# An encoder layer whose inputs are handed over turned: x, mem and Wq transposed on the host, parameters packed, the residual loaded into its accumulator

## The chip, the cores and the metric

The kernel runs on one core of a Trainium2 chip. The metric is the device time of one execution in microseconds (us). A profile of one execution tells when each engine worked: TensorE (PE; its weight loads are PEld), VectorE (DVE), ScalarE (ACT), GpSimd (POOL), and the DMA queues, of which that of SyncE (SP) issues nearly all transfers.

## The reference

One layer of a bidirectional encoder on 2048 tokens of 1024 numbers, all in float32:

```
u = rmsnorm(x) * g_mix;  P = u @ W_in                        # 1024 -> 3600 columns
hyena group: 3-tap conv of P; two long convolutions by FFT with filters made by a small sine network
mLSTM group: 3-tap conv, SiLU; chunkwise scan in both directions; sigmoid output gate
h = x + concat(groupnorm(hyena), groupnorm(mlstm)) @ w_out
h = h + softmax((rmsnorm(h) Wq)(rmsnorm(mem) Wk)^T / 16) (rmsnorm(mem) Wv) Wo     # 4 heads, 256 rows of mem
h = h + relu(rmsnorm(h) @ W1)^2 @ W2
out = rmsnorm(h)
```

x and mem come with one token per row, the weights with one input channel per row.

## The kernel before

**Products.** A product of two float32 matrices is done as three faster products of their parts (`mm3`, L293): each operand is split into a high part (a copy on ScalarE that rounds, L300) and a low part (a subtraction on VectorE, L301). A "bank" is one accumulator of 128 by 512 in TensorE's output memory; a bank of the projection takes 8 times 3 matmuls. Plain float32 matmuls, slower, are used for the FFT stages and the filters.

**Channels on partitions.** For a product TensorE wants the channels along the partitions. x and mem are stored with tokens along them, so they are turned. `prep` (L425) goes over row tiles of 128 tokens: `prep_load` (L395) loads one, `prep_norm` (L404) squares it on ScalarE with a running sum, makes 1/rms in a chain of small VectorE operations (`rsqrt`, L144) and multiplies by it and by the gain, `prep_turn` (L416) turns it in eight transposes on TensorE (L420) and splits the result into xh and xl. Half of x (1024 tokens) fits at a time, so it is prepared three times: first half, second half, first half again. `turned` (L331) does the same for Wq, four transposes (L341) for each of 16 pieces.

**Stages.** `program` (L1638) sets the order. `sweep` (L512) projects the hyena and q, k columns with the weights as they come from `stream` (L347), which loads and splits one weight pair ahead; each bank is copied, convolved on ScalarE and VectorE, turned back (L576) and stored. Between its banks the sweep pops the generator of the next preparation (L546, L550). `filters` (L158) is woven between the sweep's steps and opens a pool of its own; `hyena` (L638), `natural` (L605), `mlstm` (L771) and `memproj` (L458: products of mem with Wk and Wv, and of these with Wq and Wo) follow in the same way. `attention` (L1061) goes over four chunks of 512 tokens: w_out product, residual, norm, scores, softmax, second product. At the beginning of a chunk `residual` (L1131) loads x by rows, turns it on TensorE (`turn`, L1103, and L1106) and copies it into `acc`; `finish` (L1141) adds each bank to it, and L1243 stores it for the later stages. The feed-forward part comes last.

**Order.** The instructions are put in order by a scheduler of the framework that simulates the engines; `keep_in_program_order` exempts single instructions. Each engine and each DMA queue works strictly in its order, so a wait holds what stands behind it.

Of the kernel before, what the change touches and what calls it, by code (L numbers as in the profile page):

```python
# [9 lines left out]
F32 = mybir.dt.float32  # L10
# [86 lines left out]

class Prog:
    def __init__(self, ctx, tc, a):
# [17 lines left out]
        self.prepq = None  # L117
        self.rbp = cp.tile([128, 16], F32, name="rbp")
        self.ps = ctx.enter_context(tc.tile_pool(name="ps", bufs=1, space=PSUM))
# [38 lines left out]
    def filters(self):  # L158
# [3 lines left out]
        with tc.tile_pool(name="f_sb", bufs=1, side="right") as sb:  # L162
            def ta(bufs=7):
                return sb.tile([128, 2, CH], F32, tag="a", name="a", bufs=bufs)

            def tb(bufs=8):
                return sb.tile([128, CH], F32, tag="b", name="b", bufs=bufs)

            w1 = sb.tile([66, 128], F32, name="w1")
            w2 = sb.tile([128, 128], F32, name="w2")  # L170
            w3 = sb.tile([128, 2, CH], F32, name="w3")
            f1 = sb.tile([128, 2, 128], F32, name="f1")
            nc.vector.memset(w1, 0.0)
            nc.vector.memset(w2, 0.0)
            nc.gpsimd.dma_start(out=w1[0:33, 0:64], in_=a["hy_filt_w1"][0])
            nc.gpsimd.dma_start(out=w1[33:66, 64:128], in_=a["hy_filt_w1"][0])
            nc.gpsimd.dma_start(out=w2[0:64, 0:64], in_=a["hy_filt_w2"][0])
            nc.gpsimd.dma_start(out=w2[64:128, 64:128], in_=a["hy_filt_w2"][0])
            par = sb.tile([128, 4], F32, name="par")
            for i, n in enumerate(("b1", "freq1", "b2", "freq2")):  # L180
                src = a["hy_filt_" + n].rearrange("o c -> c o")
                for h in range(2):
                    nc.gpsimd.dma_start(out=par[64 * h:64 * h + 64, i:i + 1], in_=src)
            w3v = a["hy_filt_w3"][0].rearrange("k (o r c) -> r k o c", o=2, r=2)
            for h in range(2):
                nc.gpsimd.dma_start(out=w3[64 * h:64 * h + 64], in_=w3v[h])
            nc.gpsimd.dma_start(out=f1, in_=a["c_f1"])

            def sine(dst, src, b, fr):
                u, k = tb(), tb()  # L190
                nc.vector.tensor_scalar(u, src, par[:, b:b + 1], par[:, fr:fr + 1], ALU.add, ALU.mult)
# [6 lines left out]
                nc.vector.tensor_scalar(u, u, -PI_F, PI_F, ALU.max, ALU.min)  # L198
                nc.scalar.activation(dst, u if len(dst.shape) == 2 else u.rearrange("p (q j) -> p q j", j=16), AF.Sin)

            hid = sb.tile([128, 16, 128], F32, name="hid")
            for c in range(4):
# [7 lines left out]
                sine(hid1, p1, 0, 1)  # L210
# [8 lines left out]
            def windows(j2):  # L219
# [3 lines left out]
                for r in range(2):  # L223
                    nc.sync.dma_start(out=w[r], in_=wv[r, :, 2 * j2:2 * j2 + 2])
# [40 lines left out]
            def blocks(o, i):  # L265
                p, k = divmod(2 * i, 16)
                dm = sb.tile([128, 2, 128], F32, tag="dm", name="dm", bufs=3)
                nc.sync.dma_start(out=dm, in_=a["c_dm"][:, 2 * i:2 * i + 2])
# [6 lines left out]
            for n, (o, i) in enumerate(order):  # L275
                if True:
# [9 lines left out]
                    nc.sync.dma_start(out=hd[o, 2 * i:2 * i + 2].rearrange("k l c -> l k c"), in_=hs)  # L286

    def column(self, ap, n, name):
        t = self.cp.tile([128, n], F32, name=name, tag=name)
        self.nc.gpsimd.dma_start(out=t, in_=ap.rearrange("o (k p) -> p (o k)", p=128))  # L290
        return t
# [7 lines left out]
    def split(self, hi, lo, src):  # L299
        self.nc.scalar.copy(hi, src)  # L300
        self.nc.vector.tensor_tensor(lo, src, hi.bitcast(F32), ALU.subtract)  # L301
# [10 lines left out]
    def weights(self, pool, w, n, kc=4, bufs=2, nbufs=2):  # L312
# [12 lines left out]
        for k0 in range(0, kt, kc):  # L325
            nat = pool.tile([128, kc, n], F32, tag="wn", name="wn", bufs=nbufs)
            nc.sync.dma_start(out=nat, in_=w[128 * k0:128 * (k0 + kc), :].rearrange("(k p) c -> p k c", p=128))
            self.split(hi[:, k0:k0 + kc], lo[:, k0:k0 + kc], nat)
        return hi, lo

    def turned(self, pool, w):  # L331
        nc = self.nc
        hi = pool.tile([128, 2, 1024], F32R, tag="wh", name="wh", bufs=2)
        lo = pool.tile([128, 2, 1024], F32R, tag="wl", name="wl", bufs=2)
        for i in range(4):
            nat = pool.tile([128, 2, 256], F32, tag="wn", name="wn", bufs=3)
            nc.sync.dma_start(out=nat, in_=w[256 * i:256 * i + 256, :].rearrange("(k p) c -> p k c", p=128))
            pt = self.mm()
            for m in range(2):
                for k in range(2):  # L340
                    nc.tensor.transpose(pt[:, 256 * m + 128 * k:256 * m + 128 * k + 128],  # L341
                                        nat[:, k, 128 * m:128 * m + 128], self.ident)
            ds = slice(256 * i, 256 * i + 256)
            self.split(hi[:, :, ds], lo[:, :, ds], pt.rearrange("p (m c) -> p m c", m=2))
        return hi, lo

    def stream(self, pool, items, **kw):  # L347
        nxt = None
        for i in range(len(items) + 1):
            cur = nxt  # L350
            if i < len(items):
                w, n = items[i]
                nxt = self.turned(pool, w) if n is None else self.weights(pool, w, n, **kw)
            if cur is not None:
                yield cur
# [3 lines left out]
    def inproj_open(self, es):  # L359
# [9 lines left out]
        self.g_mix = self.bcast(sb, a["norm_mix_g"], D, "g_mix")  # L369
        self.turned_to = lambda h: (self.xh[:, 4 * h:4 * h + 4], self.xl[:, 4 * h:4 * h + 4])  # L370
        self.xh = sb.tile([128, 8, 1024], F32R, name="xh")
        self.xl = sb.tile([128, 8, 1024], F32R, name="xl")
        self.cw = sb.tile([128, 3, 20], F32, name="cw")
        self.cb = sb.tile([128, 20], F32, name="cb")
        for i in range(3):
            nc.gpsimd.dma_start(out=self.cw[:, i, 0:12], in_=a["hy_conv_w"][:, i].rearrange("o (k p) -> p (o k)", p=128))
            nc.gpsimd.dma_start(out=self.cw[:, i, 12:20], in_=a["ml_conv_w"][:, i].rearrange("o (k p) -> p (o k)", p=128))
        nc.gpsimd.dma_start(out=self.cb[:, 0:12], in_=a["hy_conv_b"].rearrange("o (k p) -> p (o k)", p=128))
        nc.gpsimd.dma_start(out=self.cb[:, 12:20], in_=a["ml_conv_b"].rearrange("o (k p) -> p (o k)", p=128))
        self.gb = sb.tile([128, 16], F32, name="gb")  # L380
        nc.gpsimd.dma_start(out=self.gb, in_=a["ml_gate_b"].broadcast_to([128, 16]))
        self.carry = sb.tile([128, 20, 17], F32, name="carry")
# [5 lines left out]
        second = [(a["xa_wq"][0][:, h], None) for h in hs] + [(a["xa_wo"][0][h, :], 1024) for h in hs]  # L388
# [4 lines left out]
        self.wst = self.stream(sb, items, kc=2, nbufs=3)  # L393

    def prep_load(self, src, first, i):  # L395
        sb = self.isb
        if first and i % 3:
            xn = sb.tile([128, 1042], F32, tag=("P", "cv")[i % 3 - 1], name="xn", bufs=2)[:, 0:D]
        else:
            xn = sb.tile([128, D], F32, tag="xn", name="xn", bufs=2)  # L400
        self.nc.sync.dma_start(out=xn, in_=src)
        return xn

    def prep_norm(self, xn, gain):  # L404
        nc, sb = self.nc, self.isb
        ss = sb.tile([128, 2], F32, tag="ss", name="ss", bufs=2)
        for h in range(2):
            junk = sb.tile([128, 512], F32, tag="st", name="junk", bufs=3)
            nc.scalar.activation(junk, xn[:, 512 * h:512 * h + 512], AF.Square, accum_out=ss[:, h:h + 1])
        ms = sb.tile([128, 1], F32, tag="ms", name="ms", bufs=2)  # L410
        nc.vector.tensor_tensor(ms, ss[:, 0:1], ss[:, 1:2], ALU.add)
        nc.vector.tensor_scalar(ms, ms, 1.0 / D, EPS, ALU.mult, ALU.add)
        rv = self.rsqrt(sb, ms, "xr")
        nc.vector.scalar_tensor_tensor(xn, xn, rv, gain, ALU.mult, ALU.mult)

    def prep_turn(self, xn, t):  # L416
        for h in range(2):
            p = self.mm().rearrange("p (k t) -> p k t", k=4)
            for k in range(4):
                self.nc.tensor.transpose(p[:, k], xn[:, 512 * h + 128 * k:512 * h + 128 * k + 128], self.ident)  # L420
            hi, lo = self.turned_to(h)
            ts = slice(128 * t, 128 * t + 128)
            self.split(hi[:, :, ts], lo[:, :, ts], p)

    def prep(self, src, gain, first=False):  # L425
        n = src.shape[0] // 128
        ahead = 5 if first else 1
        q = []
        for i in range(n + ahead):
            if i < n:  # L430
                xn = self.prep_load(src[128 * i:128 * i + 128, :], first, i)
                q.append(xn)
# [1269 lines left out]
```

## Time and profile before

| | |
|---|---|
| median of 3 runs | 3382.24 us (3379.86 to 3386.33) |
| the profiled execution | 3383.48 us, its span 3381.8 us |
| TensorE busy | 3194.3 us, 94% |
| VectorE, ScalarE, GpSimd busy | 60%, 44%, 38% |
| mean granted TensorE clock | 0.979 |

The span runs from the first to the last instruction. "Busy" of TensorE is modelled, since matmuls overlap. A row of a group gives line, engine, operation, output and input by the program's names, shapes, count, busy time, mean length of one in ns, and the idle time of the engine just before such instructions with what ended it. A row of the timeline gives start and length in us. A row of a wait gives the total in us, the number of times and the longest.

### The profile page before, as it was taken

What the parts mean: (1) busy time and instruction counts of PE and PEld (TensorE: products, weight loads), DVE (VectorE), ACT (ScalarE), POOL (GpSimd) and SP (SyncE); (2) the same over time, 40 slices, a digit from 0 to 9 for tenths busy, and PEclk for the clock granted to TensorE, in tenths of its full rate; (3) what the DMA queues carried; (4) which work ended last, traced back from release to release, by engine and by line L of the source; (5) the groups of instructions that cost most, each with busy time, mean ns of one, the idle gap of its engine ahead of it and who ended that gap; (6) DMA issues with size and microseconds to landing.
All of it is one profiled execution on the core that took longest, in us unless ns stands there. A gap on an engine that the chain in (4) does not pass through costs nothing.

```text
span 3381.8 us, 46860 instructions
## 1 busy us (share of the span) xinstructions
PE 3194.3 (94%) x15671; PEld 2550.0 (75%) x15671; DVE 2042.5 (60%) x3711; ACT 1492.4 (44%) x2884; POOL 1269.8 (38%) x894
## 2 busy tenths in 40 slices
PE   6999999999898888799999999999999999999997
PEld 5646666677676788688887997788788887888876
DVE  7685225524546755777766554755855576555695
ACT  4344435523454235444444444555655543333335
POOL 2131001200222314544424012876766564434482
PEclk9999999999999999999999999999999999999998
DMA  5366889996998579857657444765654475444434
GB/s 165 117 208 206 286 282 256 271 325 238 241 240 279 172 229 273 275 154 231 184 162 253 147 132 161 224 205 179 207 167 158 147 244 171 128 140 135 133 94 159
DMA packets 480749, 674.55 MB, mean 199 GB/s; under 512 B 41738, under 2 KB 256848, under 8 KB 479484
## 3 DMA queue, kind: packets, MB, share of 16 engines
q1 hardware_dynamic: 478904, 668.70, 63.4%
q0 software_dynamic: 1600, 2.86, 0.4%
q8 instruction: 124, 2.03, 0.3%
q14 instruction: 117, 0.96, 0.1%
q10 hardware_dynamic: 4, 0.00, 0.0%
HBM read 452.23 MB, written 219.18 MB: 199 GB/s over the span
## 4 chain that ended last, share of the span: by engine, by line
PE 43%; DVE 7%; DMA 5%; issue 3%; POOL 2%; ACT 1%; SPq 1%; DVEq 0%; ACTq 0%; POOLq 0%
PE mm L295 9%; PE mm L297 9%; PE mm L296 9%; PE hy L297 5%; PE hy L295 4%; PE hy L296 4%; DVE wl L301 1%; DVE bl L1292 1%; POOL acc L1500 1%; DMA rw<-rows 1%; PE hy L1106 1%; DMA wr<-xs 1%; DMA wn<-in_x_dram 1%; DMA va<-vd 1%; DVE acc L1542 0%
## 5 line engine op out<-in xcount | busy, mean ns | idle before, releaser
L301 DVE TENSOR_TENSOR wl<-wn,wh 128x512 fp32r<-128x512 f32 (+1 forms) x352 | 274.6, 813 | 144.4 <-ACT wh L300 143.8
L1292 DVE TENSOR_TENSOR bl<-wr,bh 128x512 fp32r<-128x512 f32 x213 | 234.8, 1108 | 134.6 <-ACT bh L1291 132.2
L1291 ACT CAST ah<-w 128x512 fp32r<-128x512 f32 x284 | 176.2, 622 | 298.9 <-PE hy L296 152.7
L300 ACT CAST wh<-wn 128x512 fp32r<-128x512 f32 (+1 forms) x352 | 202.1, 617 | 216.2 <-PE mm L296 80.0
L295 PE MATMUL mm<-xh,wh 128*128 128x512 f32 x640 | 276.4, 432 | 8.7 <-ACT P L542 7.5
L739 POOL TENSOR_TENSOR b<-b,a 128x512 f32<-128x512 f32 x64 | 88.8, 1387 | 502.1 <-ACT b L737 201.1
L296 PE MATMUL mm<-xl,wh 128*128 128x512 f32 x640 | 266.4, 416 | 0.1
L297 PE MATMUL mm<-xh,wl 128*128 128x512 f32 x640 | 264.3, 413 | 0.3 <-DVE wl L301 0.3
L1292 DVE TENSOR_TENSOR al<-w,ah 128x512 fp32r<-128x512 f32 x236 | 226.9, 963 | 59.9 <-ACT ah L1291 59.7
L1291 ACT CAST bh<-wr 128x512 fp32r<-128x512 f32 x232 | 143.4, 621 | 244.3 <-PE mm L297 180.1
L297 PE MATMUL mm<-bh,al 128*128 128x512 f32 x576 | 224.4, 392 | 8.3 <-DVE al L1292 5.7
L295 PE MATMUL mm<-bh,ah 128*128 128x512 f32 x576 | 226.0, 392 | 0.0
L296 PE MATMUL mm<-bl,ah 128*128 128x512 f32 x576 | 225.0, 391 | 0.0
L295 PE MATMUL mm<-act,wh 128*128 128x512 f32 x512 | 201.4, 397 | 6.0 <-ACT wh L300 6.0
L296 PE MATMUL mm<-act,wh 128*128 128x512 f32 x512 | 203.0, 397 | 0.0
L297 PE MATMUL mm<-act,wl 128*128 128x512 f32 x512 | 201.1, 396 | 0.0
L1149 POOL TENSOR_TENSOR ssum<-ssum,sq 128x512 f32<-128x512 f32 x56 | 80.7, 1440 | 269.7 <-ACT sq L1148 268.2
L295 PE MATMUL hy<-bh,ah 128*128 128x512 f32 x448 | 175.2, 391 | 0.0
L296 PE MATMUL hy<-bl,ah 128*128 128x512 f32 x448 | 174.6, 390 | 0.0
L297 PE MATMUL hy<-bh,al 128*128 128x512 f32 x448 | 174.6, 390 | 0.0
L295 PEld LDWEIGHTS mm<-xh,wh 128*128 128x128 f32 x640 | 122.4, 191 | 56.7 <-issue 18.0
L295 PE MATMUL hy<-xh,ah 128*128 128x512 f32 x384 | 152.8, 398 | 7.6 <-ACT ah L1291 6.8
(379 smaller groups left out, 9021.1 us busy)
## 6 DMA issues: line engine op xcount, KB each, us to landing
wr<-hc SPq DMA_DIRECT2D x224, 256.0 KB
w<-in_ff_w_dram SPq DMA_DIRECT2D x176, 256.0 KB
a<-hd SPq DMA_DIRECT2D x128, 256.0 KB
hc<-t SPq DMA_DIRECT2D x128, 256.0 KB
wn<-in_w_in_dram SPq DMA_DIRECT2D x104, 256.0 KB
hc<-q SPq DMA_DIRECT2D x96, 256.0 KB
fs<-a SPq DMA_DIRECT2D x32, 512.0 KB
a<-fs SPq DMA_DIRECT2D x32, 512.0 KB
```

The lines of the kernel that those rows point to most:

```text
L295: mm(ps, lh, rh, start=start, stop=False)
L296: mm(ps, lh, rl, start=False, stop=False)
L297: mm(ps, ll, rh, start=False, stop=stop)
L300: self.nc.scalar.copy(hi, src)
L301: self.nc.vector.tensor_tensor(lo, src, hi.bitcast(F32), ALU.subtract)
L739: nc.gpsimd.tensor_tensor(xt, xt, hi[:, m], ALU.mult)
L1106: nc.tensor.transpose(pt[:, 128 * k:128 * k + 128], yn[:, 128 * k:128 * k + 128], self.ident)
L1149: nc.gpsimd.tensor_tensor(ssum, ssum, sq, ALU.add)
L1291: self.nc.scalar.copy(hi, src)
L1292: eng.tensor_tensor(lo, src, hi.bitcast(F32), ALU.subtract)
L1500: nc.gpsimd.tensor_tensor(v, v, ms[2 * tp + n], ALU.mult)
```

## The change

The host hands over, beside x and mem, their transposes `x_t` and `mem_t`, and Wq only transposed; it packs all gains, convolution weights and biases into one array of 128 by 192 (`par`) and the filter network's weights into one of 128 by 1280 (`fw`).

- x is loaded with channels on partitions (`x_load`) and needs no turning. 1/rms of a token, which is now needed along the free dimension, is made into a diagonal matrix (`diagonal`) and spread over all partitions by one matmul with ones (`spread`); VectorE multiplies by gain and 1/rms (`gained`), and the pieces are split.
- The sums of squares come for the first 512 tokens from the turned tiles (squares added on VectorE, four matmuls with a column of ones). For the other tokens and mem they come from row tiles that are loaded beside (`row_stats`), once, in steps popped between the first banks; the third preparation reuses them.
- `x_first` writes the beginning out by hand, with most of the order pinned; the second 512 tokens are written in the middle of the first bank (`self.mid`).
- The pool of the filters is opened first, and its tiles hold the first weights and x.
- Wq goes through the ordinary `weights`.
- `residual` is one DMA of 128 by 2048 numbers straight into `acc`, which is one tile for all four chunks; in the first chunk it stands behind the turning of the mLSTM rows.
- Tiles of P and cv are 1088 wide in place of 1042; some loads of the filters are kept in program order.

```diff
-    def prep_turn(self, xn, t):
-        for h in range(2):
-            p = self.mm().rearrange("p (k t) -> p k t", k=4)
-            for k in range(4):
-                self.nc.tensor.transpose(p[:, k], xn[:, 512 * h + 128 * k:512 * h + 128 * k + 128], self.ident)
...
+    def spread(self, dg, pin=False):
+        n = dg.shape[1]
+        p = self.mm()
+        d = self.nc.tensor.matmul(p[:, 0:n], self.ones, dg, start=True, stop=True)
...
+        rb = self.isb.tile([128, 512], F32, tag="rb", name="rb", bufs=2)
+        self.nc.scalar.copy(rb[:, 0:n], p[:, 0:n])
+        return rb[:, 0:n]
+
+    def gained(self, x, g, rb):
+        return self.nc.vector.scalar_tensor_tensor(x, x, g, rb, ALU.mult, ALU.mult)
+
+    def scaled(self, x, k0, gain, rb, hi, lo):
+        for k in range(x.shape[1]):
+            self.gained(x[:, k], gain[:, k0 + k:k0 + k + 1], rb)
+        self.split(hi, lo, x)
...
+    def x_chunk(self, c):
+        rb = self.spread(self.diagonal(self.rx[:, 4 * c:4 * c + 4]))
+        xs = [self.x_load(c, 0)]
+        for j in range(4):
+            if j < 3:
+                xs.append(self.x_load(c, j + 1))
+            to = slice(2 * j, 2 * j + 2), slice(512 * (c % 2), 512 * (c % 2) + 512)
+            self.scaled(xs.pop(0), 2 * j, self.g_mix, rb, *(t[(slice(None),) + to] for t in (self.xh, self.xl)))
+            yield
...
+    def x_first(self):
...
+        for k in range(8):
+            sq = sb.tile([128, 512], F32, tag="st", name="sq", bufs=3) if k else ssum
+            pin(nc.scalar.activation(sq, x0[k], AF.Square))
+            if k:
+                nc.vector.tensor_tensor(ssum, ssum, sq, ALU.add)
+        p = self.mm()
+        for t in range(4):
+            nc.tensor.matmul(p[:, t:t + 1], ssum[:, 128 * t:128 * t + 128], self.ones[:, 0:1], start=True, stop=True)
+        self.inv_rms(self.rx[:, 0:4], p[:, 0:4])
+        dg = self.diagonal(self.rx[:, 0:4])
...
+        rb = self.spread(dg)
...
+        write(x0, c0, rb, between)
+
+        def rest():
+            write(x1, c1, self.spread(later[0], True))
+            w1 = self.weights(sb, *self.items[1], kc=2, nbufs=3, pin=True)
+            self.wst = self.stream(sb, self.items[2:], w1, kc=2, nbufs=3)
+        self.mid = rest
+        for _ in range(9):
+            yield
+        for c in (2, 3):
+            yield from self.row_stats(self.rx[:, 4 * c:4 * c + 4], self.a["x"][512 * c:512 * c + 512])
+        yield from self.row_stats(self.rm, self.a["mem"])
...
-        second = [(a["xa_wq"][0][:, h], None) for h in hs] + [(a["xa_wo"][0][h, :], 1024) for h in hs]
+        second = [(a["xa_wq_t"][h, :], 1024) for h in hs] + [(a["xa_wo"][0][h, :], 1024) for h in hs]
...
             def residual(h):
-                q = [rows(a["x"], 512 * c + 128 * t, h) for t in range(2)]
-                for t in range(4):
-                    xn = q.pop(0)
-                    if t < 2:
-                        q.append(rows(a["x"], 512 * c + 128 * (t + 2), h))
-                    self.copy(acc[:, 4 * h:4 * h + 4, 128 * t:128 * t + 128], turn(xn))
+                src = a["x_t"].rearrange("(k p) t -> p k t", p=128)[:, 4 * h:4 * h + 4, 512 * c:512 * c + 512]
+                nc.sync.dma_start(out=acc[:, 4 * h:4 * h + 4], in_=src)
...
                     half = [gemm(w, i, y, None, range(4)) for i in range(2)]
+                    next(mix)
                     residual(0)
                     residual(1)
-                    next(mix)
```

More of the change, by code (lines that the diff above doesn't have):

```diff
@@ L117, in __init__ @@
         self.prepq = None
+        self.mid = None
         self.rbp = cp.tile([128, 16], F32, name="rbp")
+        par = self.par = cp.tile([128, 192], F32, name="par")
+        nc.scalar.dma_start(out=par, in_=a["par"])
+        self.g_mix, self.g_mem, self.gx, self.gf = (par[:, 8 * i:8 * i + 8] for i in range(4))
+        self.cw = par[:, 32:92].rearrange("p (i c) -> p i c", i=3)
+        self.cb, self.gb = par[:, 92:112], par[:, 112:128]
         self.ps = ctx.enter_context(tc.tile_pool(name="ps", bufs=1, space=PSUM))
@@ L310, in bcast, with weights @@
         return t
-    def weights(self, pool, w, n, kc=4, bufs=2, nbufs=2):
+    def weights(self, pool, w, n, kc=4, bufs=2, nbufs=2, pin=False):
         nc = self.nc
@@ L327, in weights, with stream @@
             nc.sync.dma_start(out=nat, in_=w[128 * k0:128 * (k0 + kc), :].rearrange("(k p) c -> p k c", p=128))
-            self.split(hi[:, k0:k0 + kc], lo[:, k0:k0 + kc], nat)
+            self.split(hi[:, k0:k0 + kc], lo[:, k0:k0 + kc], nat, pin)
         return hi, lo
[L331 to L349, printed above, removed]
-            cur = nxt
[L351 to L355, printed above, removed]
+    def stream(self, pool, items, cur, **kw):
+        for w, n in items:
+            nxt = self.weights(pool, w, n, **kw)
+            yield cur
+            cur = nxt
+        yield cur
     NAT_AT = (0, 2, 4)
@@ L368, in inproj_open @@
         sb = self.isb = es.enter_context(tc.tile_pool(name="i_sb", bufs=1))
[L369 to L370 removed]
         self.xh = sb.tile([128, 8, 1024], F32R, name="xh")
         self.xl = sb.tile([128, 8, 1024], F32R, name="xl")
[L373 to L382, printed above, removed]
+        small = sb.tile([128, 448], F32, name="small")
+        self.carry = small[:, 0:340].rearrange("p (c t) -> p c t", c=20)
+        self.rx, self.rm = small[:, 340:356], small[:, 356:358]
         win = a["w_in"][0]
@@ L416, in prep_turn @@
-    def prep_turn(self, xn, t):
-        for h in range(2):
-            p = self.mm().rearrange("p (k t) -> p k t", k=4)
-            for k in range(4):
[L420 to L432, printed above, removed]
-            if i >= ahead:
-                xn = q.pop(0)
-                self.prep_norm(xn, gain)
-                self.prep_turn(xn, i - ahead)
-                yield
+        self.items = items
```

253 lines of the change are left out of this document (182 added, 71 removed).

## The prediction

> **What bounds the kernel now.** I read the page first, then the stretches around the places that the diff touches, then the waits, then the start instruction by instruction. The page:
>
> ```profile
> span 3381.8 us, 46860 instructions
> ...
> PE 3194.3 (94%) x15671; PEld 2550.0 (75%) x15671; DVE 2042.5 (60%) x3711; ACT 1492.4 (44%) x2884; POOL 1269.8 (38%) x894
> ...
> PE 43%; DVE 7%; DMA 5%; issue 3%; POOL 2%; ACT 1%; SPq 1%; DVEq 0%; ACTq 0%; POOLq 0%
> ```
>
> TensorE is the bound: 94% of the span, 187.5 us idle in all, and the largest share of the chain that ends last. An edit pays if it takes work from TensorE's stream or if it shortens a stretch in which TensorE waits. The stretches (columns: PE, PEld, DVE, ACT, POOL busy with instruction counts, granted TensorE clock, DMA share, GB/s):
>
> ```profile
> 0.00:60.00 60.00, 33.03 (x135) 24.59 (x136) 41.24 (x154) 28.33 (x62) 17.70 (x31) 0.97 0.72 203
> 150.00:300.00 150.00, 147.31 (x510) 76.75 (x509) 112.51 (x238) 64.01 (x125) 45.26 (x25) 1.00 0.53 181
> 800.00:900.00 100.00, 86.14 (x400) 60.05 (x399) 60.14 (x162) 45.06 (x97) 11.81 (x9) 0.91 0.87 260
> 1100.00:1150.00 50.00, 41.72 (x237) 32.83 (x235) 49.52 (x129) 9.03 (x22) 26.22 (x18) 0.90 0.55 189
> 1150.00:1280.00 130.00, 113.30 (x885) 109.39 (x884) 65.11 (x213) 42.01 (x82) 14.23 (x17) 0.93 0.68 207
> 1400.00:1450.00 50.00, 38.32 (x211) 32.31 (x210) 26.30 (x70) 17.15 (x45) 13.42 (x12) 0.86 0.82 253
> 1600.00:1640.00 40.00, 36.47 (x192) 30.23 (x191) 25.20 (x57) 16.46 (x42) 13.96 (x11) 0.96 0.66 211
> 1790.00:1830.00 40.00, 31.76 (x145) 25.04 (x144) 20.88 (x28) 14.92 (x26) 19.50 (x14) 0.91 0.99 329
> ```
>
> The first 60 us hold 27 us of TensorE's idle time. The stretch 150 to 300 is full of TensorE work. The other six are the places where x is prepared a second time (800), mem is prepared (1100), Wq is turned (1150) and the residual is turned (1400, 1600, 1790): in all of them TensorE has gaps and a granted clock below 1.
>
> **What goes from TensorE.** The groups (busy, mean ns of one, idle before) and the 64 turns of Wq:
>
> ```profile
> L420 PE MATMUL mm<-ident,xn 128*128 128x128 f32 x208 | 33.2, 304 | 30.6 <-DVE xr_t L153 16.5 <-DVE hr_t L154 5.8 <-DVE xr_t L154 4.7
> L1106 PE MATMUL hy<-ident,wn 128*128 128x128 f32 x256 | 39.4, 296 | 19.2 <-DMA wn<-in_x_dram 9.8 <-DMA wn<-yh 7.6 <-DMA wn<-ym 1.4
> L734 PE MATMUL hy<-a,dm 128*128 128x512 f32 x128 | 68.6, 622 | 8.7 <-DMA a<-zs 6.8 <-issue 1.9
> L341 PE MATMUL mm<-ident,wn x64: 270/273/448, 1172.3 to 1271.2; 128*128 128x128 f32 x64
> ```
>
> All 208 transposes of L420 go (3 times 64 for x, 16 for mem), all 64 of L341, and 128 of the 256 of L1106 (4 chunks, 2 halves, 4 rows, 4 each): 400. The means overlap, since transposes are pipelined; a run of twelve took 1.47 us (row at 52.46 below), 0.12 each, less the tail of the last, so I count 0.11 each in a full stream: 44 us. By busy time (33.2/208) it is 0.16 each, 64 us; that is the upper bound.
>
> What comes: seven matmuls that spread 1/rms over the partitions, six of 512 columns and one of 256, in f32. L734 is that operation: 64 matmuls (two instructions each) in 68.6 us, 1.07 each, so 7 us in all, and four tiny ones. Net 37 us off TensorE.
>
> **1. The start (edits: x handed over turned, pool of the filters opened first, packed parameters).** TensorE's stream, and when ScalarE could square the row tiles of x:
>
> ```profile
> 10.16 1.94 PE L420 MATMUL mm<-ident,xn 128*128 128x128 f32 x8 [10.16 <-DVE xr_t L153]
> ...
> 30.75 1.38 PE L295 MATMUL mm<-xh,wh 128*128 128x512 f32 x1
> ...
> 44.38 0.50 PE L295 MATMUL mm<-xh,wh 128*128 128x512 f32 x1 [2.78 <-ACT P L542]
> 44.72 0.39 PE L296 MATMUL mm<-xl,wh 128*128 128x512 f32 x1
> 44.95 0.39 PE L297 MATMUL mm<-xh,wl 128*128 128x512 f32 x1
> ...
> 52.46 1.47 PE L420 MATMUL mm<-ident,xn 128*128 128x128 f32 x12
> ...
> 74.19 1.91 PE L576 MATMUL mm<-ident,cv 128*63 128x128 f32 x16
> ```
>
> ```profile
> 4.35 0.63 ACT L409 ACTIVATE junk<-xn 128x512 f32<-128x512 f32 x1 [2.26 <-DMA xn<-in_x_dram]
> ...
> 13.96 0.63 ACT L409 ACTIVATE junk<-xn 128x512 f32<-128x512 f32 x1 [2.54 <-DMA xn<-in_x_dram]
> ```
>
> ```profile
> DMA packets 1043, 3.03 MB, mean 216 GB/s; under 512 B 312, under 2 KB 312, under 8 KB 1043
> ```
>
> At 74.19 the first four banks of the projection are done (matmuls of a bank start 0.23 apart, 24 of them are 5.6 us, four are 22.4) and the first result is turned: the mark that I compare. The new first chunk is four loads of 512 KB, as large as the four row tiles whose fourth was there at 13.96, while 3.03 MB moved in the first 14 us. The packed weights of the filters (655 KB on POOL's queue) stand where the 512 KB of the broadcast gain stood. So x is whole at about 14 us again. Then, in a chain:
>
> ```profile
> 5.72 0.16 DVE L411 TENSOR_TENSOR ms<-ss 128x1 f32<-128x1 f32 x1 [4.34 <-ACT junk L409]
> 5.92 0.15 DVE L412 TENSOR_SCALAR ms<-ms 128x1 f32<-128x1 f32 x1
> ...
> 52.66 0.81 DVE L191 TENSOR_SCALAR b<-hy,par 128x512 f32<-128x512 f32 x1 [1.84 <-PE hy L212]
> ...
> 58.36 0.43 DVE L198 TENSOR_SCALAR b<-b 128x512 f32<-128x512 f32 x1
> ```
>
> ```profile
> L301 DVE TENSOR_TENSOR wl<-wn,wh 128x512 fp32r<-128x512 f32 (+1 forms) x352 | 274.6, 813 | 144.4 <-ACT wh L300 143.8
> L301 DVE TENSOR_TENSOR xl<-mm,xh 128x512 fp32r<-128x512 f32 x48 | 31.8, 683 | 4.0 <-ACT xh L300 3.9
> L414 DVE SCALAR_TENSOR_TENSOR xn<-xn,xr_y,g_mix 128x1024 f32<-128x1024 f32 x24 | 32.2, 1343 | 0.7 <-DMA g_mix<-in_norm_mix_g_dram 0.4
> L300 ACT CAST xh<-mm 128x512 fp32r<-128x512 f32 x48 | 26.4, 589 | 14.5 <-PE mm L420 14.4
> ```
>
> Last square 0.6, last add 0.7, four column sums 0.6 (no row; an estimate from the transposes, 0.24 each at 10.16, less overlap), thirteen small VectorE operations 0.2 apart (rows at 5.72 and 5.92) 2.5, four diagonals 0.8 (an estimate, 0.2 each as for the small ones), the spread matmul 1.1 (L734) and its copy 0.6 (L300), first gain 0.7 (half of L414), first copy 0.6: 8.2, so the first real matmul stands at 22 to 23 in place of 30.75. From there VectorE sets the pace: a gain and a subtraction, two at 0.68, for each of 16 pieces, 22 us, and in between the sums of the second chunk (fourteen small ones and a diagonal, 3.5) and one set of the sine (3.5, six operations between L191's 0.81 and L198's 0.43). 22.5 + 29 = 51.5, plus the filters' f32 matmuls that also stand before 74.19 (about four, 1.07 each): 56. Gain 18, of which 7 are the 64 transposes. Bounds: VectorE at 0.81 for each piece and another sine set, 68 (gain 6); everything overlapped but the chain, 48 (gain 26). The pinned instructions only say which goes first; the pinned window loads wait behind pieces of x in the same buffers, but the filters need them late.
>
> **2. x, second half (150 to 300).** 64 transposes, 7 us, less two spreads, 2.1: 5. TensorE is busy for 98% there, so it counts in full; bounds 3 and 8 (at 0.16 each). VectorE has less: a chunk now costs it 16 pieces, 11 to 13 us, where four row tiles cost four chains of 2.5, four multiplications of 1.34 and eight subtractions of 0.68, 21 us.
>
> **3. x, first half again (800 to 900).** The same 5; above it up to 8 more of the 14 us idle there, below it nothing, as DMA is at 0.87. I take 5.
>
> **4. mem (1100 to 1150).** 16 transposes less half a spread: 1. The statistics move to the start's idle ScalarE, so the chain in front of the transposes goes; its wait was 5.8 (row L420, hr_t). I take 4 together, bounds 0 and 9.
>
> **5. Wq handed over turned (1150 to 1280).** 7 us of transposes, and the waits in front of them:
>
> ```profile
> PE mm L341 <- DMA wn<-in_xa_wq_dram: 7.8, 5, 3.2
> PE mm L341 <- DVE pad L823: 2.5, 1, 2.5
> PE mm L341 <- DVE cb L910: 1.9, 1, 1.9
> ```
>
> The DMA's wait can move to the copies of the same weights, the VectorE ones (4.4) go with the transposes: 11, bounds 3 and 19.
>
> **6. The residual by DMA.** 128 transposes, 14 us, and 32 copies on ScalarE and VectorE. The waits for in_x (9.8, row L1106) go as far as nothing follows them; 2048 KB a chunk come as before, in two loads that wait for the accumulator to be free:
>
> ```profile
> 1577.97 0.37 SPq L1243 DMA_DIRECT2D h<-acc  x1
> ...
> 1611.53 0.32 SPq L1243 DMA_DIRECT2D h<-acc  x1
> ```
>
> The second half is free after the store at 1611.53, and its load is needed five banks (28 us) later. TensorE can run four banks ahead, 22 us, before a late first half stops it, but the add that waits holds VectorE's queue, with the next weights' subtractions behind it. I take 14 plus half the waits, 5, less 3 for that: 16. Bounds 6 (a 3 us stall at each chunk) and 26.
>
> The small parameter loads that are packed, and the tiles at equal offsets, I cost at nothing: the only wait for one of them in the rows above is 0.4 on VectorE (L414, g_mix). If the packed load came late, the first gain would be late by as much; it has 20 us.
>
> In sum 18 + 5 + 5 + 4 + 11 + 16 = 59. The profiled execution took 3383.5 (its span and 1.7 around it), 1.2 above the median of the runs, by which every time below is lowered: 3383.5 - 59 - 1.2 = 3323. All low bounds, 18, give 3364; all high ones, 101, give 3281.
>
> A rule that speaks against the change: VectorE's subtraction takes 813 ns from SBUF and 683 from PSUM (rows L301), and the change makes some 104 pieces (16 for each of six and a half chunks) read twice from SBUF. The Trainium skill, page "SBUF — State Buffer", section "Who interferes with whom", says that a VectorE instruction with two SBUF inputs contends with a GpSimd one that reads SBUF, and that the later one is blocked altogether. The trace agrees in the sign. By that rule 104 times 0.13, 14 us, come back if all were on the path, and the sum is 45; by the rows VectorE is the pace only at the start, where POOL is idle, so I leave it at 59.
>
> **The rivals.**
> A, as above: 3323, own range 3305 to 3345, chance 0.60.
> B, hidden anyway: in the stretches at 800 and 1100 to 1280 other things (DMA at 0.87, 0.68) set the time, and VectorE's pace eats the start: 6 + 5 + 0 + 0 + 3 + 16 = 30, 3352, chance 0.18. For it: TensorE idles there already. Against: the waits named are those of the transposes.
> C, the clock comes back too: the six stretches with transposes lose (1 - clock) times their length: 9 + 5 + 9 + 7 + 1.6 + 3.6 = 35. Eight transposes at 10.16 took 0.24 each, twice the 0.12 at 52.46. If turning lowers the clock, 59 + 35 = 94: 3288, chance 0.12. Against: most of the loss stands beside waits that stay.
> The Trainium skill, page "TensorE: Matmul & The Clock Gate", section "Part 4: PE-mode transpose", states this rule: transposes don't count as activity for the clock gate. The rate at 52.46 speaks against it.
> D, slower: the loads into the accumulator are issued on SP's queue right behind the first store, and the second waits there for the second store, 33.6 us later; behind it stand the weights. With one pair of weights in hand (two banks, 11.2) TensorE stops for 22.4 at each of three boundaries, 67: 3390. It decides from 22 us at each (59 + 7 over 3). Chance 0.05. For it: the queue is in order. Against: the load stands behind the first bank in the program.
> E, no change, the same with stops of some 20 us: 0.05. That the transposes stay in can't be: no call of them is left.
>
> **The numbers.** Faster means below 3375.5, slower above 3389: 0.2% (6.8 us) is about what a measurement of this kernel can tell from no change. A, B and C are faster, 0.90; E 0.05; D 0.05. The range takes in A, B and most of C and leaves out D and E: 3288 to 3366.
>
> **What would show it.** TensorE's instructions fall by about 390. First projection matmul at 21 to 24, the first turned result (74.19 now) at 48 to 68. No wait in front of TensorE for x, xr or Wq chains; in the stretch of the residual, TensorE's idle time down by 5 to 10 us and the loads of x into the accumulator landing before the bank that needs them. SP's queue not held for over 10 us by those loads. I am wrong if the mark at the start moves by under 6 us, or if idle time in front of the projections of mem, Wq or the first banks of a chunk grows by what the transposes took.

## The result, and the profile after

The changed kernel takes 3352.95 us (median of 6 runs, 3346.61 to 3358.46), the kernel before beside it 3381.05 (6 runs): ratio 0.9911, 95% interval 0.9894 to 0.9928. It is faster by 28 us, about half of the 59 forecast. The profiled execution took 3358.12 us, 25.4 less than the profiled one of before. The page of the changed kernel (span, busy time by engine, the chain by engine):

```profile
span 3356.4 us, 45646 instructions
...
PE 3171.6 (94%) x15293; PEld 2518.0 (75%) x15293; DVE 2039.8 (61%) x3469; ACT 1469.7 (44%) x2811; POOL 1262.9 (38%) x868
...
PE 69%; DMA 15%; DVE 9%; issue 3%; ACT 2%; SPq 1%; POOL 1%; DVEq 0%; ACTq 0%; POOLq 0%
```

TensorE has 378 instructions less, but only 22.7 us less of busy time where 37 were counted, and it idles as long as before (184.8 against 187.5 us). The transfers' share of the chain has gone from 5% to 15%. TensorE's stream at the start of the changed kernel, and VectorE's last subtraction for x there:

```profile
24.00 0.79 PE L323 MATMUL mm<-xh,wh 128*128 128x512 f32 x1 [2.11 <-ACT xh L483]
...
28.30 0.63 PE L323 MATMUL mm<-xh,wh 128*128 128x512 f32 x1
28.73 1.90 PE L226 MATMUL hy<-b,fw 66*128 66x512 f32 x2
...
35.04 2.08 PE L230 MATMUL hy<-b,fw 128*128 128x512 f32 x2 [3.24 <-ACT b L217]
37.46 0.79 PE L323 MATMUL mm<-xh,wh 128*128 128x512 f32 x1 [0.35 <-ACT xh L483]
...
39.63 1.91 PE L440 MATMUL mm<-dg,ones 128*128 128x512 f32 x2
...
43.90 0.51 PE L325 MATMUL mm<-xh,wl 128*128 128x512 f32 x1
...
67.64 1.91 PE L706 MATMUL mm<-ident,cv 128*63 128x128 f32 x16
```

```profile
53.52 0.68 DVE L485 TENSOR_TENSOR xl<-a,xh 128x512 fp32r<-128x512 f32 x1
```

The first projection matmul has come forward from 30.75 to 24.00, and the mark (first turned result) by about as much, 6.6 us, from 74.19 to 67.64. The same stretches as in the prediction, in the changed kernel (same columns):

```profile
0.00:60.00 60.00, 35.98 (x109) 24.07 (x110) 45.44 (x104) 30.43 (x58) 1.97 (x8) 0.91 0.53 186
...
1150.00:1280.00 130.00, 121.82 (x970) 118.72 (x969) 72.35 (x220) 48.05 (x91) 18.66 (x19) 0.97 0.72 224
1400.00:1450.00 50.00, 42.19 (x210) 35.01 (x210) 37.05 (x66) 22.93 (x55) 18.83 (x15) 0.93 0.67 207
1600.00:1640.00 40.00, 39.01 (x185) 32.60 (x186) 30.00 (x55) 17.39 (x43) 17.83 (x13) 0.91 0.61 189
1790.00:1830.00 40.00, 31.44 (x156) 26.82 (x154) 30.18 (x28) 17.23 (x30) 26.73 (x19) 0.91 0.76 239
```

Where the time came from is seen best by asking when the same piece of work starts in both traces. Three groups mark the front of the kernel; each row gives shortest, median and longest in ns, then the first and the last start. The last step of the filters, then the middle and the last product of the hyena stage, first before, then after:

```profile
L284 PE MATMUL hy<-a,dm x128: 590/592/667, 310.1 to 456.6; 128*128 128x512 f32 x128
L734 PE MATMUL hy<-a,dm x128: 590/592/1190, 529.5 to 1051.1; 128*128 128x512 f32 x128
L753 PE MATMUL hy<-a,e x128: 590/592/1061, 715.1 to 1129.1; 128*128 128x512 f32 x128
```

```profile
L306 PE MATMUL hy<-a,dm x128: 590/592/595, 367.7 to 487.4; 128*128 128x512 f32 x128
L864 PE MATMUL hy<-a,dm x128: 590/592/1061, 564.4 to 1051.3; 128*128 128x512 f32 x128
L883 PE MATMUL hy<-a,e x128: 590/592/1222, 752.1 to 1128.5; 128*128 128x512 f32 x128
```

The filters are done 31 us later than before, and the hyena stage ends where it ended (1129.1 and 1128.5). All that the edits gave in the first 1100 us is gone. Behind that point the gain arises: the first rows of the mixed input are turned at 1407.8 before and 1392.2 after (16 us, in the stretch of mem and Wq), the first feed-forward product starts at 2087.0 and 2062.5 (9 more, in the stretch of the residual), and nothing more comes to the end.

Such marks of one execution are not exact. The experiments have two kernels (the residual alone, Wq alone) whose order of TensorE's instructions is that of the kernel before up to 1172 us. Their rows of the last product of the hyena stage, the residual's first:

```profile
L753 PE MATMUL hy<-a,e x128: 590/592/1012, 715.8 to 1132.3; 128*128 128x512 f32 x128
L753 PE MATMUL hy<-a,e x128: 590/592/1055, 721.4 to 1143.4; 128*128 128x512 f32 x128
```

With the same order the stage ended at 1129.1, 1132.3 and 1143.4. A difference of under some 14 us in this mark, between two executions, says nothing.

The projections went the other way: with their banks counted from 0, bank 20 starts at 292.7 before and at 225.5 after. The written order of TensorE's instructions shows the same: the last front matmul of the filters (L238, now L258) stands behind 21 banks of projections before, behind 29 after. The weights with which the program weaves filters and sweeps (230 to 200) are the same; the scheduler made another order of it. The hyena stage needs the filters' results and moves much data (the stretches before and after; columns as above):

```profile
300.00:600.00 300.00, 294.29 (x1148) 201.47 (x1147) 105.68 (x153) 134.93 (x223) 19.92 (x15) 1.00 0.87 275
600.00:1100.00 500.00, 464.81 (x2113) 334.91 (x2112) 240.76 (x453) 217.00 (x381) 83.98 (x60) 0.96 0.90 266
```

```profile
300.00:600.00 300.00, 293.52 (x1081) 190.47 (x1080) 102.45 (x150) 126.98 (x207) 23.15 (x15) 0.99 0.80 261
600.00:1100.00 500.00, 459.96 (x2049) 324.80 (x2048) 239.98 (x370) 213.94 (x358) 95.46 (x66) 0.97 0.95 279
```

With the filters late, the transfers have less to do until 600 us (0.80 of their time, 0.87 before) and are nearly full after it (0.95, 0.90 before). Theory 1 of the experiments is read from these rows: the change let the projections run ahead of the filters, and a stage that is limited by its transfers began too late. Theory 2: the sums of work and transfers set the end of that stage, whatever the order.

### The profile page after: what moved, and what is told of

Its sections match the earlier page's. It is cut to its first block, busy times and chain, and to the rows that moved or that the text cites. A ratio compares the mean times of both kernels' runs of the same rounds, so it can differ in the third digit from the quotient of the medians.

```text
span 3356.4 us, 45646 instructions
## 1 busy us (share of the span) xinstructions
PE 3171.6 (94%) x15293; PEld 2518.0 (75%) x15293; DVE 2039.8 (61%) x3469; ACT 1469.7 (44%) x2811; POOL 1262.9 (38%) x868
## 4 chain that ended last, share of the span: by engine, by line
PE 69%; DMA 15%; DVE 9%; issue 3%; ACT 2%; SPq 1%; POOL 1%; DVEq 0%; ACTq 0%; POOLq 0%
PE mm L324 14%; PE mm L323 14%; PE mm L325 14%; PE hy L325 5%; PE hy L323 5%; PE hy L324 5%; DMA a<-hd 4%; DVE wl L328 2%; PE hy L258 2%; PE hy L306 1%; PE hy L850 1%; PE hy L883 1%; DVE bl L1415 1%; DMA rw<-rows 1%; DMA a<-zs 1%
## 5 line engine op out<-in xcount | busy, mean ns | idle before, releaser
L328 DVE TENSOR_TENSOR wl<-wn,wh 128x512 fp32r<-128x512 f32 (+1 forms) x364 | 290.2, 832 | 121.9 <-ACT wh L328 121.3
L328 ACT CAST wh<-wn 128x512 fp32r<-128x512 f32 (+1 forms) x364 | 208.4, 618 | 208.8 <-DMA wn<-in_w_in_dram 86.2
L324 PE MATMUL mm<-xl,wh 128*128 128x512 f32 x640 | 276.5, 432 | 0.4 <-DVE xl L485 0.4
L282 POOL TENSOR_TENSOR b<-b 128x512 f32<-128x512 f32 x32 | 66.3, 2073 | 283.8 <-DVE b L277 141.7
```

Source lines behind the costliest of these rows:

```text
L282: nc.gpsimd.tensor_tensor(e[1], f, b, ALU.subtract)
L324: mm(ps, lh, rl, start=False, stop=False)
L328: both = (self.nc.scalar.copy(hi, src), self.nc.vector.tensor_tensor(lo, src, hi.bitcast(F32), ALU.subtract))
```

## The experiments

The kernel before ran beside each set, with medians from 3381 to 3392 us; so ratios to it are compared, with their 95% intervals. The difference of two ratios has the root of the sum of the squared half-widths as its half-width.

**The order of the filters, in the changed kernel and in the old one.**

```diff
-            weave(p.filters(), s, 230, 200)
+            weave(p.filters(), s, 700, 200)      # changed kernel, then the kernel before; 160 and 500 in two more
```

> The changed kernel with one number changed: the weight by which the emission of the filters is woven with the first two sweeps of projections goes from 230 to 700, so that in the written order of TensorE the filters' last front matmul stands behind 18 banks of projections in place of 29 (the kernel before: 21). No work is added or left out. Theory 1, the change let the projections run ahead of the filters, the hyena stage behind the filters starts later and is limited by its transfers, so the time won by 300 us is lost before 1100 us: with the filters ahead some 10 to 20 us come back, 3333 to 3343. Theory 2, the hyena stage's end is set by the sum of the work or of the transfers, whatever the order: within 4 us of the changed kernel's 3353.

Measured: 3327.02 us, ratio 0.9821 (0.9798 to 0.9844). One number, no work added or left out, and the gain is 0.0179 of 3381, 61 us. Against the changed kernel's own order it is 0.0090 ± 0.0029, 30 us, more than the 10 to 20 of theory 1. Its rows of the same three groups:

```profile
L306 PE MATMUL hy<-a,dm x128: 590/592/596, 282.7 to 400.8; 128*128 128x512 f32 x128
L864 PE MATMUL hy<-a,dm x128: 590/592/1222, 502.5 to 1035.9; 128*128 128x512 f32 x128
L883 PE MATMUL hy<-a,e x128: 590/592/697, 686.1 to 1110.1; 128*128 128x512 f32 x128
```

The filters end 87 us earlier than in the changed kernel, the hyena stage 18 us earlier. Theory 2 falls. In the four later runs that also have the 700 in the changed kernel, the stage ends between 1094.2 and 1104.8, so the 18 us are not the accident of one execution.

> The kernel before with the same number changed the other way, 230 to 160: in the written order the filters' last front matmul stands behind 30 banks of projections in place of 21, about where the changed kernel has it (29). Theory 1 (late filters hold up the hyena stage): slower than before by 10 to 20 us, 3391 to 3401. Theory 2 (the sums set the end): within 4 us of 3381.

Measured: 3397.33 us, ratio 1.0035 (1.0023 to 1.0047): 12 us slower, inside the range of theory 1 by its lower half. The filters end at 489.5. The hyena stage ends at 1137.6, 8.5 later than before, which by itself is within the spread of that mark. The transfers moved as in the changed kernel: 0.78 of their time from 300 to 600 us and 0.94 from 600 to 1100, against 0.89 and 0.88 in the changed kernel with 700.

> The kernel before with the weave's weight at 700, as in the run that put the filters ahead in the changed kernel: the filters' last front matmul stands behind 19.5 banks of projections in place of 21. Theory 1, the order that the kernel before had was already a good one and it is the change that lost it: within 5 us of before. Rival, the 700 is worth some 25 us whatever kernel it is put in, and says nothing of the change: 0.993 of before, about 3357 where before takes 3381.

Measured: 3382.77 us, ratio 0.9997 (0.9981 to 1.0013). The 700 is worth nothing in the old kernel: its filters end at 418.7 in place of 456.6, and its hyena stage does not end earlier (1141.6; the transfers' shares stay at 0.87 and 0.89). So the 700 gives its 30 us only together with the change, whose own order had lost them. Late filters cost 12 us in the old kernel and 30 in the changed one; why it is more there isn't shown.

> The changed kernel with the weave's weight at 500: the filters' last front matmul stands behind 22.75 banks of projections, between 18 (0.982 of before) and the changed kernel's own 29 (0.991). Theory, the time follows the filters' place in the order: 0.985 to 0.987. Rival, only another accident of the order made the run with 700 fast: no relation, 0.991 or more.

Measured: 3339.12 us, ratio 0.9857 (0.9817 to 0.9897), as the theory has it; the rival's 0.991 lies outside the interval, the 0.9821 of the run with 700 inside. The filters end at 437.5, and the hyena stage at 1110.7, as with 700. So filters that end at 487 to 490 cost time in both kernels, and no gain is shown from ending them still earlier than 440 to 457 (this run against the one with 700, and the old kernel with 700).

**Is the hyena stage limited by its transfers?** In the changed kernel with its own order:

```diff
+            if i == 0:
                 dm = sb.tile([128, 2, 128], F32, tag="dm", name="dm", bufs=2)
                 em = sb.tile([128, 2, 128], F32, tag="em", name="em", bufs=2)
                 nc.sync.dma_start(out=dm, in_=a["c_dm"][:, 2 * i:2 * i + 2])
                 nc.sync.dma_start(out=em, in_=a["c_em"][:, 2 * i:2 * i + 2])
+                held_dm[:] = [dm, em]
+            dm, em = held_dm
```

> The changed kernel with its own order (weight 230), but the middle part of the hyena stage loads its pair of constant blocks once for each of the two orders and uses them for all 16 steps: 60 loads of 128 KB, 7.9 MB, are left out, and the hyena results are those of wrong constants; all matmuls and everything else are as in the changed kernel. Theory, that stage is limited by its transfers (their share is 0.94 and 0.97 of the time from 600 to 1100 us): at the 280 GB/s of that stretch the loads are 28 us of transfers, and 12 to 28 us go, 0.983 to 0.988 of before. Rival, it is the chain from one step to the next, or TensorE: less than 5 us, 0.990 or more.

Measured: 3338.77 us, ratio 0.9854 (0.9815 to 0.9893), 19 ± 14 us less than the changed kernel. The last product of the stage and the second stretch of this run:

```profile
L888 PE MATMUL hy<-a,e x128: 590/592/1005, 732.1 to 1104.8; 128*128 128x512 f32 x128
```

```profile
600.00:1100.00 500.00, 477.56 (x2172) 341.60 (x2171) 258.76 (x413) 217.74 (x364) 101.58 (x72) 0.98 0.92 274
```

The filters end as late as in the changed kernel, but the stage ends 24 us earlier, and TensorE is busy for 17.6 us more of the 500. With that order the stage is limited by its transfers; the same loads were not left out with the filters ahead.

**The parts alone, and taken back.** The residual's edit of the diff shown above, in the kernel before:

> The kernel before with one edit alone: x is also handed over turned, and the residual is loaded into a single accumulator by DMA, with the loads after the second half of the first mixed chunk; 128 transposes and 32 copies go. The forecast priced this at 16 us (bounds 6 and 26): 3381 - 16 = 3365. The lead of the changed kernel's TensorE work over the old one's grew by only some 8 us between 1400 and 2100 us of the span: by that reading the term is 8, 3373. If the gain of one part depends on what the other parts leave, neither holds, and the time says how much the part is worth with nothing else changed.

Measured: 3379.39 us, ratio 0.9973 (0.996 to 0.9985): 9 us, not 16.

> The kernel before with Wq alone handed over turned: 64 transposes go, its weights come in the form of the other 1024-column weights. The forecast priced this at 11 us (bounds 3 and 19): 3370. The lead grew by some 7 us between 1130 and 1280 us of the span and gave back as much by 1450 us, where the split of the output weights is waited for: by that reading 0 to 7, 3374 to 3381.

The edit is the one line of `second` in the diff above. Measured: 3381.61 us, ratio 0.9986 (0.9971 to 1.0): 5 us, between 0 and 10.

> The kernel before with the residual by DMA, Wq handed over turned and the weight at 700: what is missing against the changed kernel with the filters ahead (0.982 of before) is x and mem handed over turned, the packed parameters and the pool. The forecast priced x and mem at 18 + 5 + 5 + 4 = 32 us: this kernel should then stand 32 us above that one, at 0.9915. If residual and Wq are worth only what they gave alone (9 and 5) and 700 gives nothing here, it stands at 0.996, and x and mem are worth 46.

The kernel before with both of these edits and the weight 700. Measured: 3368.51 us, ratio 0.9944 (0.9924 to 0.9965). x and mem, with the packed parameters and the pool, are worth 0.0123 ± 0.0031, 42 ± 10 us, once the order is right: the 32 forecast is at the edge of that. Residual and Wq together are worth 0.0053 ± 0.0026 here, 18 us, where they gave 14 one by one.

> The changed kernel with the filters ahead (weight 700) and the residual put back: rows of x, 128 transposes, 32 copies, one accumulator for each chunk. The forecast's term of 16 us: 0.9868 of before. The 9 us that the edit gave alone: 0.985. If what goes is only TensorE's time for the transposes, 14 us, with nothing behind them: 0.986.

The changed kernel with 700 and the old `residual`. Measured: 3338.8 us, ratio 0.9862 (0.9833 to 0.9891): the residual is worth 14 ± 13 us. The three readings can't be told apart by this run.

**Where the first residual is loaded.**

```diff
         acc = T.tile([128, 8, 512], F32, name="acc")
+        for h in range(2):
+            nc.sync.dma_start(out=acc[:, 4 * h:4 * h + 4],
+                              in_=a["x_t"].rearrange("(k p) t -> p k t", p=128)[:, 4 * h:4 * h + 4, 0:512])
         mix = mixed(0)
...
-                    residual(0)
-                    residual(1)
```

> The changed kernel with the filters ahead (weight 700), and the first chunk's two residual loads written before its first rows, not after the second half of the mixed chunk. Theory, in the changed kernel these 2 MB stand ahead of the output weights on the queue and in the engines, and TensorE waits 5.5 and 1.8 us for the split of those weights: 5 to 7 us come back, 0.980 of before. Rival, the same bytes only move to a stretch whose transfers are at 0.93 of their time already and delay other loads: 0.982, or worse.

Measured: 3329.59 us, ratio 0.9832 (0.9803 to 0.9861): no gain is shown (0.0011 ± 0.0037 above the run with 700, so the times don't exclude a small one). The waits of TensorE, with the filters ahead, and then with this load early as well:

```profile
PE mm L323 <- ACT wh L328: 17.5, 9, 3.9
...
PE hy L1233 <- DMA wn<-yh: 8.5, 1, 8.5
```

```profile
PE hy L1233 <- DMA wn<-yh: 14.3, 1, 14.3
...
PE mm L323 <- ACT wh L328: 9.8, 8, 2.8
```

The wait for the split of the weights falls by 7.7 us, and the wait for the rows of yh rises by 5.8. In these two executions the same bytes stand in front of another load, as the rival has it.

**The start.**

```diff
-            if k == 4:
+            if k == 7:
                 self.close_sums(self.rx[:, 4:8], ss)
...
-                sine(hid1, p1, 0, 1, c == 0)
+                sine(hid1, p1, 0, 1)
```

> The changed kernel with the filters ahead (weight 700), and at the start the sums of the second chunk closed after the last piece of the first chunk in place of the fifth, and the first sine's first operation not pinned: the written order of VectorE then has the eight gains of the first chunk before the sine and the small operations, which stood there 6 us long between the sixth gain and the seventh. Theory, VectorE's held-up pieces are what starves TensorE between 31 and 39 us and keeps it at half rate until 44: the first turned result of the projections (66.3 in the run with the filters ahead) comes 4 to 7 us earlier. Rival, TensorE's half rate after a pause is what costs, wherever the pause stands: the pause moves to the second chunk, the mark moves by less than 2 us.

Measured: 3326.32 us, ratio 0.9819 (0.9776 to 0.9861); the mark is at 65.7, 0.5 us earlier. The theory falls, and the pause moved as the rival has it: TensorE now waits 2.67 us up to 37.08, for the sine, and behind that the matmuls start 0.43 apart again until 42.9.

```diff
+        warm(16)        # 16 matmuls of ident with ones, 128 columns, behind the first column sums
...
         rb = self.spread(dg)
+        warm(8)
```

> The run before this one (start reordered, filters ahead) with 24 matmuls of 128 columns, identity times ones, added on TensorE where it waits for VectorE: 16 behind the first column sums and 8 behind the first spread; nobody reads them. Theory, the first projections run at 0.43 us each in place of 0.23 from 24.1 to 28.7 because TensorE has just idled: with TensorE busy ahead of them they run at 0.23 sooner and the mark comes some 2 us earlier than in that run. Rival, the rate rises at a time of its own or f32 matmuls of 128 columns don't raise it: the mark stays within 0.5 us, or comes later by what the added matmuls hold up.

Measured: 3328.98 us, ratio 0.9819 (0.9773 to 0.9866); the mark is at 66.1. TensorE's stream in this run:

```profile
15.58 5.74 PE L531 MATMUL mm<-ones,ident 128*128 128x128 f32 x32
...
25.36 0.40 PE L325 MATMUL mm<-xh,wl 128*128 128x512 f32 x1
25.59 0.40 PE L323 MATMUL mm<-xh,wh 128*128 128x512 f32 x1
26.28 0.51 PE L324 MATMUL mm<-xl,wh 128*128 128x512 f32 x1 [0.29 <-DVE xl L485]
```

The first projections do run at full rate now, and each piece waits 0.29 us for VectorE's subtraction: the mark stays. The half rate of the first projections was real, but hidden behind VectorE. The second stretch at half rate, behind the sine's pause (granted clock 0.5 from 36.7 to 43.5), is still in this run; no run is without it.

The version to keep is the changed kernel with the weight at 700: 0.9821 of before. Neither edit of the start shows a gain on top of it.

## Why the prediction was right or wrong

**The time** lies in the range, 30 us above the forecast, and it does so in part by luck: the loss that brought it there stands in no term of the sum. It is the number of rival B (3352), but not B's account: B had 11 us from the first two steps, 3 from Wq and nothing from the third step and mem, because other things would hide the rest. The traces show nothing left of the first three steps at 1128 us, and some 30 us come back when one number of the order is changed.

**The step that failed** is the second, and with it the first and the third: "TensorE is busy for 98% there, so it counts in full". TensorE's freed time did count, for the projections; what was late next was not asked. The projections ran ahead, the filters fell back by eight banks in the written order, and the stage behind them is limited by transfers. The 28 us of the first three steps were there and were given back: with the filters ahead, x and mem are worth 42 ± 10, against 32 for them in the sum. Why the scheduler set the order so is not shown by any run. From bank 12 to bank 20 it took 158 us before (134.3 to 292.7) and takes 103 after, but that doesn't show that the turning of x's second half held projections back: with 700 the same banks take 160 us (120.9 to 280.6) without any turning.

**1, the start.** The chain was right: first projection matmul at 24.0 (22 to 23 forecast). VectorE's pace was nearly right: the last piece at 54.2 (51.5). The mark was wrong, 67.6 in place of 56; the gain of 6.6 is the low bound, and just over the 6 that the forecast set as the sign of being wrong. The mis-sized term is TensorE's own work, which was taken to end with VectorE's pieces. The forecast counted four banks of projections ahead of the mark; in both traces 120 projection matmuls stand between the first of them and the mark, which is five banks, 28 us at full rate. From first matmul to mark the trace shows 43.6 us, 43.4 before. The 32 transposes that went from this stretch had 4.9 us of it; in their place the projections take 2.8 us more (0.43 apart until 43.9), the filters' matmuls 2.1 and the spread 0.9, and pauses take 0.8 less. Neither VectorE's held-up pieces nor the half rate of the first projections set the mark alone, as the last two runs show.

**4 and 5, mem and Wq.** 4 + 11 forecast; from the last hyena product to the first turned rows it is 278.7 us before and 263.7 after, 15.0. That is the sum forecast, but it isn't shown: in the old kernel with 700, which has neither edit, the same stretch took 264.1, so one execution can't tell. By its time Wq alone gave 5 (0 to 10), where 11 was forecast; mem alone was not run.

**6, the residual.** 16 forecast; 9 in the changed kernel by the marks, 9 alone (5 to 14), 14 ± 13 taken back. The waits for in_x are gone, as forecast, but 2 MB of loads now stand ahead of the first output weights: from 1330 to 1480 us TensorE waits 7.2 us for the split of weights, 5.8 with the residual's edit alone, and not at all before. (The wait for yh was there before, 7.6 us, and is 7.7 after.) TensorE's idle time in the three stretches fell from 23.5 to 17.4 us, within the 5 to 10 forecast. The term that was too large is then the 5 us of waits that were to go for good; this is read from the traces, and moving the first load did not bring the time back.

**The rivals.** C: the mean granted clock is 0.976 (0.979 before); taking 400 transposes away brought none of it back. D: the loads into the accumulator are issued 8.8 and 5.4 us behind the stores (1562.13 and 1570.95, 1595.90 and 1601.29), and TensorE doesn't wait for them.

**The price of a subtraction from SBUF.** At the start, with POOL busy for 2 of 60 us, L485 takes 0.68 to 0.69 us with both inputs in SBUF, as the 683 from PSUM; L328's mean over the kernel is 832, with POOL at work. Sorted by what ran beside them, the 262 subtractions of L328 during which no GpSimd instruction ran took 0.69 in the median and at most 0.73; the 102 during which one ran took 1.2 in the mean and up to 1.8. So the difference of 0.13 comes from what runs beside, not from where the data lie. The rule of the Trainium skill, page "SBUF — State Buffer", section "Who interferes with whom", agrees with that. The 14 us worked out by it could not be charged at the start, where POOL is idle.

## What to carry to other kernels

Where a scheduler sets the order, an edit that frees one stream moves the others: compare the written order and the ends of the stages before and after, not only the busy times. When a gain is missing, look for the first place where the same work stands later than before; here one number in the weave brought 30 us back. Read such marks beside the medians of the times: with one and the same order a mark moved by 14 us between executions. Work that a transfer-bound stage waits for goes first, even where TensorE is full.

## What the runs showed of the hardware

Two matmuls of the filters that use opposite halves of the partitions (64 rows each) run side by side when they stand next to each other in TensorE's stream, and one after the other when another matmul stands between. Both kinds in the changed kernel:

```profile
204.35 0.69 PE L273 MATMUL hy<-fw,hid 64*128 64x512 f32 x1
204.36 0.69 PE L274 MATMUL hy<-fw,hid 64*128 64x512 f32 x1
...
211.67 1.12 PE L273 MATMUL hy<-fw,hid 64*128 64x512 f32 x2
...
213.16 1.12 PE L274 MATMUL hy<-fw,hid 64*128 64x512 f32 x2
```

The pair at 204.35 takes 1.06 us (the next instruction starts at 205.41), the split one 1.06 for each. Of the 32 pairs, 15 ran side by side before, 9 after and 23 with the filters ahead: by that, an estimate, the order itself costs TensorE 6 us more after than before and 15 more than with the filters ahead. How much of the 30 us this is stays open. It is hardly the whole: the halfway run has 15 such pairs, and its hyena stage ends as early as with 23; the old kernel with late filters has 18, more than before, and is slower; and the run with fewer loads has 8 and gains 19 us.

In the run with the added matmuls, these start 0.213 us apart for the first 4.0 us and 0.112 apart from then on; eight column sums stand right ahead of them, from 13.85. In the kernel before, transposes at 28.09 start 0.213 apart and those at 31.96, 3.9 us of unbroken work later, 0.11; only 2.1 us of that work are matmuls (from 29.82). In the changed kernel unbroken matmuls from 24.00 on still start 0.43 apart at 28.73, 4.7 us later, so 2.1 us of matmuls alone were not enough there. This speaks for the transposes having counted towards the rise. The Trainium skill, page "TensorE: Matmul & The Clock Gate", section "Part 4: PE-mode transpose", which the prediction weighed under C, says that they don't count in the same way; the trace speaks against it for these f32 transposes.
